# A rotary embedding on one core: three VectorE operations for five slabs, four stores as even and odd partitions, and a tile for each place of a slab

## The chip, the cores and the metric

The kernel runs on one core of a Trainium2 chip. The metric is the device time in microseconds (us) of one execution. Before the change it is 162.14 us, the median of three runs (162.01 to 162.23).

## The reference

`x` is float32 of 16 x 512 x 1024 (batch, sequence, dim): 33.5 MB to read, and as much to write. A row of 1024 is 16 heads of 64. In every head the first 32 numbers and the last 32 are turned against each other by tables that depend on the place in the sequence only:

```python
x = x.reshape(batch, seq, num_heads, head_dim)          # 16 x 512 x 16 x 64
x1, x2 = x[..., :half_dim], x[..., half_dim:]
cos = cos[None, :, None, :]                             # 512 x 32
sin = sin[None, :, None, :]
rotated = np.concatenate([x1 * cos - x2 * sin,
                          x1 * sin + x2 * cos], axis=-1)
```

## The kernel before

The work is cut into eight slabs of two batches, 4 MB each. A slab lies on 128 partitions with eight rows of 1024, so 32 KB of float32, on each. Slabs go in pairs: the two slabs of a pair take alternate runs of 32 KB in DRAM.

On chip, one tile `room` of 192 KB a partition holds six places ("slots") of one float32 slab each. `halves` is the same memory seen as bfloat16, so that a slot is also two halves (numbers 2i and 2i+1) which hold one bfloat16 slab each. Three tuples say where a slab lies: `land[s]` is the slot that its load fills, `home[s]` the half in which its bfloat16 form lies, `leave[s]` the slot from which it is stored as float32.

The steps of a slab:

- `load(s, r, n)` (L83) brings rows r to r+n of slab s into its slot, on SyncE's queue.
- `cast(s)` (L154) on ScalarE makes bfloat16 of it: `land` to `home`.
- `turn(s)` on VectorE does the arithmetic in bfloat16, for four of the eight rows at a time: a product of the swapped halves with the sine table into `turned_part`, a tile called `spare` in the profile (L168), a product with the cosine table in place (L168), and the sum in place (L171). That is six operations of 128 x 4096 for a slab.
- `spread(s)` (L158) on ScalarE makes float32 of it, `home` to `leave`, and then issues `store(s)` (L87), again on SyncE's queue. Slab 1 is spread and stored in two pieces of four rows.

The tables come in once: two loads of 64 KB, on ScalarE's queue, to 32 partitions four apart; GpSimd casts them, eight matmuls (L145) copy them to all partitions, and VectorE brings them from PSUM to bfloat16 (L150). They do not enter the loop again.

The order of the instructions on ScalarE, VectorE and SyncE is the order in the code (`tc.manual_schedule`). Loads 0 to 5 are issued at the start; load 6 goes to slot 2 after cast 2, load 7 (in pieces of six rows and two) to slot 3 after cast 3. Store 0 has a dependency of its own on load 7's first piece (`gate`), so that no store is under way before the loads are nearly through. All these transfers are on one queue, SyncE's.

Of the kernel before, what the change touches and what calls it, by code (L numbers as in the profile page):

```python
# [9 lines left out]
@with_exitstack  # L10
def kernel(
    ctx: ExitStack,
    tc: tile.TileContext,
    x: bass.AP,
    cos: bass.AP,
    sin: bass.AP,
    num_heads: int,
    out: bass.AP,
):
    nc = tc.nc  # L20
    P = nc.NUM_PARTITIONS

    batch, seq, dim = x.shape
    nh = num_heads
    hd = dim // nh
    half = hd // 2
    bf16 = mybir.dt.bfloat16
    f32 = mybir.dt.float32

    nb = 2  # L30
    slots = 6
    TAIL = 2
    nslabs = batch // nb
    G = 2
    rpp = nb * seq // P
    W = rpp * dim
    SP = seq // rpp
    TW = rpp * half

    out_flat = out.rearrange("b s h d -> b s (h d)")  # L40

    singles = ctx.enter_context(tc.tile_pool(name="singles", bufs=1))
    psum = ctx.enter_context(tc.tile_pool(
        name="psum", bufs=1, space=bass.MemoryType.PSUM))


    def dram(t, s, k):
        return bass.AP(tensor=t.tensor,
                       offset=t.offset + s // G * (G * nb * seq * dim) + s % G * W,
                       ap=[[G * W, P], [1, k * W]])  # L50


    def view(t, offset, *dims):
        return dataclasses.replace(t, offset=t.offset + offset,
                                   ap=[t.ap[0], *[list(d) for d in dims]])


    room = singles.tile([P, slots * W], f32, tag="room")
    halves = room.bitcast(bf16)


    land = (0, 1, 2, 3, 4, 5, 2, 3)
    home = (0, 1, 2, 3, 8, 9, 0, 1)
    leave = (5, 2, 5, 1, 2, 4, 5, 0)


    def rows(t, s, r, n):
        return bass.AP(
            tensor=t.tensor,
            offset=t.offset + s // G * (G * nb * seq * dim) + s % G * W + r * dim,  # L70
            ap=[[G * W, P], [1, n * dim]])


    def wide(slot, r, n):
        return view(room, slot * W + r * dim, (1, n * dim))


    def thin(s, r, n):
        return view(halves, home[s] * W + r * dim, (1, n * dim))


    def load(s, r, n):
        return nc.sync.dma_start(out=wide(land[s], r, n), in_=rows(x, s, r, n))  # L83


    def store(s, r, n):
        return nc.sync.dma_start(out=rows(out_flat, s, r, n), in_=wide(leave[s], r, n))  # L87

    TR = 32
    TQ = seq // TR // rpp
    TC = seq * half // TR
    spare = singles.tile([P, rpp // 2 * dim // 2], f32, tag="spare")
    turned_part = spare.bitcast(bf16)
    raw = view(spare, 0, (1, TC))
    nc.vector.memset(raw, 0.0)  # L97


    def load_tables(queue):  # L100
        for i, src in enumerate((cos, sin)):
            to = dataclasses.replace(
                raw, offset=raw.offset + i * raw.ap[0][0],
                ap=[[P // TR * raw.ap[0][0], TR], [1, TC]])
            queue.dma_start(out=to, in_=bass.AP(  # L105
                tensor=src.tensor, offset=src.offset, ap=[[TC, TR], [1, TC]]))


    load(0, 0, rpp)
    load_tables(nc.scalar)  # L110
    for s in range(1, slots):
        load(s, 0, rpp)

    GP = SP // G
    GT = G // TQ
    pick = singles.tile([P, 3 * GT * P], bf16, tag="pick")
    nc.gpsimd.memset(pick, 0.0)  # L119


    def selection(g, h):
        return pick[:, (g * GT + h // TQ) * P:(g * GT + h // TQ + 1) * P]


    for g in range(3):
        for h in range(0, G, TQ):
            part = view(selection(g, h), 0, (GP, P // GP), (1, GP))
            nc.gpsimd.affine_select(  # L129
                out=part, in_=part, compare_op=mybir.AluOpType.not_equal,  # L130
                fill=-1.0 if g == 2 else 1.0,
                base=-(1 if g else 0) - h // TQ * (P // TR),
                pattern=[[0, P // GP], [-(G // TQ) * (P // TR), GP]],
                channel_multiplier=1)

    raw_b = singles.tile([P, TC], bf16, tag="raw_b")
    nc.gpsimd.tensor_copy(out=raw_b, in_=raw)  # L137

    tab = {}


    def table(h):
        acc = psum.tile([P, 2 * rpp * hd], f32, tag=f"acc{h}")
        for g, at in ((0, 0), (0, half), (2, rpp * hd), (1, rpp * hd + half)):
            nc.tensor.matmul(  # L145
                view(acc, at, (hd, rpp), (1, half)), selection(g, h),
                view(raw_b, h % TQ * TW, (half, rpp), (1, half)),
                start=True, stop=True)
        tab[h] = singles.tile([P, 2 * rpp * hd], bf16, tag=f"tab{h}", name="tab")
        nc.vector.tensor_copy(out=tab[h], in_=acc)  # L150


    def cast(s, r=0, n=rpp):
        nc.scalar.copy(out=thin(s, r, n), in_=wide(land[s], r, n))  # L154


    def spread(s, r=0, n=rpp):
        nc.scalar.copy(out=wide(leave[s], r, n), in_=thin(s, r, n))  # L158
        return store(s, r, n)


    def turn(s):
        n = rpp // 2
        for r in (0, n):
            low = thin(s, r, n)
            flip = view(low, half, (hd, n * nh), (-half, 2), (1, half))
            for out_, in_, a in ((turned_part, flip, rpp * hd), (low, low, 0)):
                nc.vector.tensor_mul(  # L168
                    out=out_, in0=in_,
                    in1=view(tab[s % G], a + r * hd, (hd, n), (0, nh), (1, hd)))  # L170
            nc.vector.tensor_add(out=low, in0=low, in1=turned_part)  # L171


    with tc.manual_schedule(engines={
            mybir.EngineType.Activation, mybir.EngineType.DVE, mybir.EngineType.SP}):
        n = rpp // 2
        cast(0, 0, n)
        cast(0, n, n)
        for h in range(G):
            table(h)  # L180
        turn(0)
        cast(1)
        turn(1)
        cast(2)
        load(6, 0, rpp)
        turn(2)
        cast(3)
        gate = load(7, 0, rpp - TAIL)
        load(7, rpp - TAIL, TAIL)
        turn(3)  # L190
        cast(4)
        cast(5)
        first = spread(0)
        tc.add_manual_dep(
            first.ins, gate.ins.name,
            mybir.DependencyInfo(mybir.DependencyClass.Sync,
                                 mybir.DependencyReason.DATA),
            reason="behind the loads")
        turn(4)
        cast(6)  # L200
        spread(1, 0, n)
        spread(1, n, n)
        turn(5)
        spread(2)
        spread(3)
        spread(4)
        turn(6)
        cast(7)
        turn(7)
        spread(5)  # L210
        spread(6)
        spread(7)


# [33 lines left out]
```

## Time and profile before

| What | Before |
|---|---|
| Runs | 162.23, 162.01, 162.14 us; median 162.14 |
| The profiled execution | 162.36 us, with a span of 160.6 us: 1.8 us lie around the span |
| VectorE busy | 112.8 us (70%), 51 instructions |
| ScalarE busy | 113.5 us (71%), 19 instructions |
| TensorE, GpSimd busy | 1.9 us and 2.1 us |
| DMA | 67.25 MB, mean 419 GB/s over the span; SyncE's queue alone is 97.4% of what 16 DMA engines can be busy |
| Transfers on SyncE's queue | 9 for the loads, 9 for the stores |

The profile is of one execution. Its busy times are of instructions on the compute engines; transfers are counted apart, as packets on 16 DMA engines. The share of a transfer queue in the table is the time of its packets over 16 engines and the span, so that 100% means that every DMA engine had a packet at every moment. In a short window that share can come out over or under 1, since a packet counts in the window in which it starts.

### The profile page before, as it was taken

To read this page: it belongs to the slowest core of one execution; us is meant where nothing else is said; L and a number is where in the kernel's file an instruction comes from. 1 tells how busy PE (TensorE), PEld (TensorE's weight loads), DVE (VectorE), ACT (ScalarE), POOL (GpSimd) and SP (SyncE) were. 2 spreads that over 40 slices of the span, in tenths; PEclk is the share of its full clock that TensorE was granted. 3 is DMA by queue.
4 is the path that set the end of the run, shared out by engine and by line. 5 is a ranking of instruction groups with operands and counts; after the bars stand their busy time and mean duration, and the time that the engine had idled before them with its cause. 6 is when DMAs were issued, how large, how long until landed. Compare 5 with 4: busy or idle time off the path is not lost.

```text
span 160.6 us, 195 instructions
## 1 busy us (share of the span) xinstructions
PE 1.9 (1%) x8; PEld 1.1 (1%) x8; DVE 112.8 (70%) x51; ACT 113.5 (71%) x19; POOL 2.1 (1%) x9
## 2 busy tenths in 40 slices
PE   0004000000000000000000000000000000000000
PEld 0002000000000000000000000000000000000000
DVE  1002999999999999999999999999739990000000
ACT  3006949488493966999999799999999999800000
POOL 3001000000000000000000000000000000000000
DMA  7999999999999999999899999999999999999993
GB/s 261 408 408 408 506 392 392 498 416 392 490 424 392 473 441 392 457 392 465 375 506 416 392 441 473 392 433 482 392 433 475 392 416 498 392 392 514 400 392 139
DMA packets 2689, 67.25 MB, mean 419 GB/s; under 512 B 320, under 2 KB 320, under 8 KB 384
## 3 DMA queue, kind: packets, MB, share of 16 engines
q1 hardware_dynamic: 2592, 67.11, 97.4%
q10 hardware_dynamic: 96, 0.13, 0.2%
q14 instruction: 1, 0.01, 0.0%
HBM read 33.69 MB, written 33.55 MB: 419 GB/s over the span
## 4 chain that ended last, share of the span: by engine, by line
DVE 62%; ACT 13%; DMA 7%; issue 3%; PE 1%; POOLq 0%; ACTq 0%; DVEq 0%
DVE room L171 20%; DVE room L168 20%; DVE spare L168 20%; ACT room L158 9%; DMA spare<-in_sin_dram 7%; ACT room L154 4%; DVE tab L150 1%; PE acc L145 1%; POOLq L243 0%; ACTq L105 0%; DVE spare L97 0%; DVEq L168 0%; POOLq L137 0%; ACTq L158 0%
## 5 line engine op out<-in xcount | busy, mean ns | idle before, releaser
L154 ACT CAST room<-room 128x8192 bf16<-128x8192 f32 (+1 forms) x9 | 56.3, 6259 | 22.6 <-DMA room<-in_x_dram 22.5
L158 ACT CAST room<-room 128x8192 f32<-128x8192 bf16 (+1 forms) x9 | 56.0, 6258 | 1.3 <-DMA out_dram<-room 1.0
L168 DVE TENSOR_TENSOR spare<-room,tab 128x4096 bf16<-128x4096 bf16 x16 | 36.7, 2292 | 4.5 <-ACT room L154 3.6
L168 DVE TENSOR_TENSOR room<-room,tab 128x4096 bf16<-128x4096 bf16 x16 | 36.7, 2292 | 0.5
L171 DVE TENSOR_TENSOR room<-room,spare 128x4096 bf16<-128x4096 bf16 x16 | 36.7, 2292 | 0.5
L150 DVE CAST tab<-acc 128x1024 bf16<-128x1024 f32 x2 | 2.4, 1220 | 13.6 <-PE acc L145 13.6
L154 ACT ACT_TABLE_LOAD x1 | 1.3, 1283 | 2.6 <-issue 2.6
L145 PE MATMUL acc<-raw_b,pick 128*128 128x256 bf16 x8 | 1.9, 416 | 13.9 <-POOL raw_b L137 13.9
L145 PEld LDWEIGHTS <-pick 128*128 128x128 bf16 x8 | 1.1, 139 | 14.2 <-issue 12.2
L97 DVE MEMSET spare<- 128x512 f32 x1 | 0.5, 485 | 0.9 <-PEq L229 0.9
L129 POOL TENSOR_SCALAR_AFFINE_SELECT pick<-pick 128x128 bf16<-128x128 bf16 x3 | 0.8, 308 | 0.1
L137 POOL CAST raw_b<-spare 128x512 bf16<-128x512 f32 x1 | 0.6, 610 | 11.2 <-DMA spare<-in_sin_dram 11.2
L119 POOL MEMSET pick<- 128x384 bf16 x1 | 0.4, 417 | 0.3 <-POOLq L229 0.3
L229 POOL MEMSET const-bfloat16-1.0<- 128x1 bf16 x1 | 0.1, 101 | 0.0
L229 POOL MEMSET const-uint8-127<- 128x1 uint8 x1 | 0.1, 101 | 0.0
L229 POOL MEMSET const-float32-0.0<- 128x1 f32 x1 | 0.1, 98 | 0.2 <-issue 0.2
L229 POOL MEMSET const-float32-1.0<- 128x1 f32 x1 | 0.1, 98 | 0.0
## 6 DMA issues: line engine op xcount, KB each, us to landing
room<-in_x_dram SPq DMA_DIRECT2D x7, 4096.0 KB, 31.7
out_dram<-room SPq DMA_DIRECT2D x7, 4096.0 KB, 14.8
out_dram<-room SPq DMA_DIRECT2D x2, 2048.0 KB, 9.9
room<-in_x_dram SPq DMA_DIRECT2D x1, 3072.0 KB, 29.4
room<-in_x_dram SPq DMA_DIRECT2D x1, 1024.0 KB, 31.5
spare<-in_cos_dram ACTq DMA_DIRECT2D x1, 64.0 KB, 7.9
spare<-in_sin_dram ACTq DMA_DIRECT2D x1, 64.0 KB, 11.1
```

Source lines behind the costliest of these rows:

```text
L97: nc.vector.memset(raw, 0.0)
L119: nc.gpsimd.memset(pick, 0.0)
L129: nc.gpsimd.affine_select(out=part, in_=part, compare_op=mybir.AluOpType.not_equal, fill=-1.0 if g == 2 else 1.0, base=-(1 if g else 0) - ...
L137: nc.gpsimd.tensor_copy(out=raw_b, in_=raw)
L145: nc.tensor.matmul(view(acc, at, (hd, rpp), (1, half)), selection(g, h), view(raw_b, h % TQ * TW, (half, rpp), (1, half)), start=True, sto ...
L150: nc.vector.tensor_copy(out=tab[h], in_=acc)
L154: nc.scalar.copy(out=thin(s, r, n), in_=wide(land[s], r, n))
L158: nc.scalar.copy(out=wide(leave[s], r, n), in_=thin(s, r, n))
L168: nc.vector.tensor_mul(out=out_, in0=in_, in1=view(tab[s % G], a + r * hd, (hd, n), (0, nh), (1, hd)))
L171: nc.vector.tensor_add(out=low, in0=low, in1=turned_part)
L229: nc = _bacc.Bacc("TRN2", target_bir_lowering=False, num_devices=1)
```

## The change

- `room` becomes a list of six tiles, one a slot. `half_place(h, r, n)` gives rows of half h; the view of a slab in a slot or half is otherwise what it was.
- For slabs 0, 1, 2, 5 and 7 a free half, named in `aside`, takes the product of the swapped halves, and `turn` does all eight rows in three operations of 128 x 8192. Slabs 3, 4 and 6 keep `turned_part` and six operations.
- Since half 10, the first of slot 5, is slab 0's `aside`, load 5 is issued after `turn(0)`. Loads 6 and 7 change slots (3 and 2 for 2 and 3): load 6 stands behind cast 3, and load 7 behind `turn(2)`, which uses half 4 of slot 2. Cast 3 goes to half 3, which is slab 1's `aside`, so it stands behind `turn(1)`. `leave` changes for slabs 1 and 4, from slot 2 to slot 3.
- Cast 0 is one instruction of 128 x 8192 in place of two of 128 x 4096; in ScalarE's order, cast 3 now stands ahead of load 6, and casts 4 and 5 ahead of `turn(3)` in the code.
- `twice(s)` stores slabs 2, 3, 4 and 5 in two transfers each: partitions 0, 2, 4, ... and then 1, 3, 5, ... (64 each), with 32 KB for a partition as before. There are 13 transfers for the stores in place of 9.

```diff
-    room = singles.tile([P, slots * W], f32, tag="room")
-    halves = room.bitcast(bf16)
-    land = (0, 1, 2, 3, 4, 5, 2, 3)
+    room = [singles.tile([P, W], f32, tag=f"room{i}", name="room") for i in range(slots)]
+    halves = [t.bitcast(bf16) for t in room]
+    land = (0, 1, 2, 3, 4, 5, 3, 2)
     home = (0, 1, 2, 3, 8, 9, 0, 1)
-    leave = (5, 2, 5, 1, 2, 4, 5, 0)
+    aside = {0: 10, 1: 3, 2: 4, 5: 1, 7: 4}
+    leave = (5, 3, 5, 1, 3, 4, 5, 0)
...
+    def half_place(h, r, n):
+        return view(halves[h // 2], h % 2 * W + r * dim, (1, n * dim))
...
+    def every_other(t, i):
+        (step, count), rest = t.ap[0], t.ap[1:]
+        return dataclasses.replace(t, offset=t.offset + i * step,
+                                   ap=[[2 * step, count // 2], *rest])
+
+    def twice(s, r=0, n=rpp):
+        for i in (0, 1):
+            nc.sync.dma_start(out=every_other(rows(out_flat, s, r, n), i),
+                              in_=every_other(wide(leave[s], r, n), i))
...
-    for s in range(1, slots):
+    for s in range(1, slots - 1):
         load(s, 0, rpp)
...
     def spread(s, r=0, n=rpp):
         nc.scalar.copy(out=wide(leave[s], r, n), in_=thin(s, r, n))
-        return store(s, r, n)

     def turn(s):
-        n = rpp // 2
-        for r in (0, n):
+        n = rpp if s in aside else rpp // 2
+        for r in range(0, rpp, n):
             low = thin(s, r, n)
             flip = view(low, half, (hd, n * nh), (-half, 2), (1, half))
-            for out_, in_, a in ((turned_part, flip, rpp * hd), (low, low, 0)):
+            crossed = half_place(aside[s], 0, n) if s in aside else turned_part
+            for out_, in_, a in ((crossed, flip, rpp * hd), (low, low, 0)):
                 nc.vector.tensor_mul(
                     out=out_, in0=in_,
                     in1=view(tab[s % G], a + r * hd, (hd, n), (0, nh), (1, hd)))
-            nc.vector.tensor_add(out=low, in0=low, in1=turned_part)
+            nc.vector.tensor_add(out=low, in0=low, in1=crossed)
...
-        cast(0, 0, n)
-        cast(0, n, n)
         for h in range(G):
             table(h)
+        cast(0)
         turn(0)
+        load(5, 0, rpp)
         cast(1)
         turn(1)
         cast(2)
+        cast(3)
         load(6, 0, rpp)
         turn(2)
-        cast(3)
         gate = load(7, 0, rpp - TAIL)
         load(7, rpp - TAIL, TAIL)
-        turn(3)
         cast(4)
         cast(5)
-        first = spread(0)
+        turn(3)
+        spread(0)
+        first = store(0, 0, rpp)
...
         turn(4)
         cast(6)
-        spread(1, 0, n)
-        spread(1, n, n)
+        for r in (0, n):
+            spread(1, r, n)
+            store(1, r, n)
         turn(5)
-        spread(2)
-        spread(3)
-        spread(4)
+        for s in (2, 3, 4):
+            spread(s)
+            twice(s)
         turn(6)
         cast(7)
         turn(7)
-        spread(5)
-        spread(6)
-        spread(7)
+        for s in (5, 6, 7):
+            spread(s)
+            (twice if s == 5 else store)(s, 0, rpp)
```

4 lines of the change are left out of this document (2 added, 2 removed).

## The prediction, made before the changed kernel ran

> **What bounds the kernel now.** I read the page first: the two rows of engines, the slices, the DMA queues.
>
> ```profile
> DVE  1002999999999999999999999999739990000000
> ACT  3006949488493966999999799999999999800000
> ...
> DMA  7999999999999999999899999999999999999993
> ...
> q1 hardware_dynamic: 2592, 67.11, 97.4%
> q10 hardware_dynamic: 96, 0.13, 0.2%
> q14 instruction: 1, 0.01, 0.0%
> ```
>
> VectorE (DVE) and ScalarE (ACT) stop five to seven slices of 4 us before the end; the DMA engines are full from the second slice to the last but one. SyncE's queue q1 fills 97.4% of the span. q14 is a packet of none of the kernel's transfers, an instruction fetch, and will matter. The page's chain of work that ended last reads "DVE 62%", which misleads: its last piece is ScalarE's cast at 132.92, 7.02 us long. It follows instructions and ends 20 us early. What ends last is a transfer, as SyncE's own waits say:
>
> ```profile
> SPq L87 <- ACT room L158: 58.1, 8, 13.5
> ...
> SPq L87 <- DMA room<-in_x_dram: 28.6, 1, 28.6
> SPq L243 <- DMA out_dram<-room: 19.2, 1, 19.2
> ```
>
> The last line is the end of the program (L243), which waits 19.2 us for the last store. The stores' waits for ScalarE (58.1 us) cost nothing while the queue still has packets. Whether it always has is seen by stage, with windows cut where loads end (81.2) and store 3 lands (119.9); the last two numbers are the DMA share and GB/s.
>
> ```profile
> 0.50:81.20 80.70, 1.87 (x8) 1.11 (x8) 65.48 (x31) 55.97 (x10) 1.86 (x5) 1.00 0.99 424
> 81.20:119.90 38.70, 0.00 (x0) 0.00 (x0) 34.52 (x16) 37.67 (x8) 0.00 (x0) 1.00 1.01 434
> 119.90:159.50 39.60, 0.00 (x0) 0.00 (x0) 12.76 (x6) 19.84 (x3) 0.00 (x0) 1.00 0.95 411
> ```
>
> Two equal amounts of work: stores 0 to 3 in 38.7 us, stores 4 to 7 in 39.6. The lost 0.9 us has an owner. Each DMA engine takes a row of 32 KB in 1213 ns, one after the other, so that a 4 MB slab is eight rows deep, 9.7 us. At 120.92 one engine also takes the fetch, an 8192 byte packet of 309 ns, and its rows on both sides take 1516 and 1571 ns. It stays behind: of store 4's 16 completion counts, 15 are in at 129.55, the last at 130.53; of the last store's, 158.66 and 159.49. So 15 engines idle for the final 0.83 us. The rest is 1.74 us until the first packet, and 1.1 us from the last count to the end of the span. Nothing else is left to gain.
>
> **The change, part by part.** The profiled execution took 162.36 us, 0.22 over the median.
>
> *VectorE's three operations.* The rows by shape:
>
> ```profile
> L154 ACT CAST room<-room 128x8192 bf16<-128x8192 f32 x7 | 49.1, 7018 | 13.2 <-DMA room<-in_x_dram 13.1
> ...
> L171 DVE TENSOR_TENSOR room<-room,spare 128x4096 bf16<-128x4096 bf16 x16 | 36.7, 2292 | 0.5
> ...
> L154 ACT CAST room<-room 128x4096 bf16<-128x4096 f32 x2 | 7.2, 3605 | 9.4 <-DMA room<-in_x_dram 9.4
> ```
>
> No 8192 operation of VectorE is shown. Above, it is two of 2292 ns, 4.58 us; below, ScalarE's ratio for the same two sizes (7018/3605 = 1.95) gives 4.46. I take 4.46, as the double size is what both share. A slab is then 3 x (4.46 + 0.03 between) = 13.5 us for 6 x 2.325 = 13.95: 0.45 us on each of five slabs, 2.3 us in all, and none of it on the path, since the queue sets the end. So the times by which transfers can be issued must be walked through for loss. Cast 0 whole: 13.29 + 7.02 = 20.3 (turn 0 began at 17.23). Turns 0, 1, 2 end at 33.9, 47.4, 60.9. Load 5 now waits for turn 0, with load 6 and all else queued behind it on SyncE: issued at 33.9, and the queue has load 4 until 51.95. Cast 3 waits for turn 1 (its half): 47.4 to 54.5; load 6 follows at 54.5, the queue lasts to 61.66. Loads 7 wait for turn 2: 60.9 against 71.4. Casts 4 (to 61.5) and 5 (data at 61.66) are then where they were, and with them ScalarE's whole later order; store 0 still goes out at 78.7 at its gate. Turn 5 must wait for the half that spread 1 frees at 90.0 (VectorE is there at 88.9), ends at 103.5, turn 6 at 117.5; turn 7 begins when cast 7 ends, 118.9, and ends at 132.4, before ScalarE is free for spread 7 at 132.8. Stores 2 to 7 go out as now at 98.0, 105.1, 112.0, 125.8, 132.8 and 140.0, against queue ends of 100.6, 110.2, 119.9, 129.2, 138.8 and 148.5. From issue to first packet took 1.01 us at the start (0.73 to 1.74). The thinnest cover is store 2's: 2.5 less 1.0, so 1.5 us. The sum for all this is 0; if a step is later than its cover, what goes beyond it is added to the end.
>
> *Fewer instructions.* VectorE issues 15 fewer. Who asked for the fetch at 120.92? SyncE had issued nothing since 112.4. ScalarE's cast at 118.78 is the 33rd of its 40 records in the trace, VectorE's product at 118.91 the 59th of 68. I take VectorE: if the engines' programs are cut alike, only it comes as far as 59. Its 68 become about 53 and it never gets there, unless six or more new waits are recorded as instructions of their own (now it has about a dozen). Saved: the final lag, 0.83 us; 0 if it was ScalarE's, which keeps 39. [...]
>
> *Stores 2 to 5 in two transfers.* Four more issues on SyncE, 0.33 us each, behind a wait for ScalarE and 2.5 us or more ahead of need: 0. One more completion packet of 9 ns per engine for each, 0.04 us. Semaphores recur after eight transfers, so later ones wait for earlier ones to have landed: the tightest is store 5's, which need store 1 (100.6) at 125.8. The speed of 64 partitions two apart is the open cost. Nearest rows: store 1 in two pieces, 4.83 us each, so a split alone is free; and the table loads, 32 partitions four apart on all 16 engines: every 2 KB packet 84 ns, and the 32 KB rows around them still 1213. I take 1213 ns, because those packets show spaced partitions with no delay, to them or to their neighbours; the other end (two engines at one group of partitions, half speed) is +38.6, below. A gain below 1213 is excluded: that is the time of a row in loads and stores, split or whole, alike.
>
> *The tail.* After the last count SyncE goes through five waits on pairs of semaphores, 0.065 us apart, and the last store's stands first. With 13 stores it falls on the eighth semaphore, whose pair stands last: 0 to 0.26 us saved; I take the middle, 0.13. Six tiles for one move no byte: 0, unless a wait comes with it that the covers above don't hold.
>
> Sum: 162.36 - 0.83 - 0.13 + 0.04 = 161.44 for a profiled execution, less 0.22 for the median: **161.2 us** (alone, 160.9 to 161.6).
>
> **The rivals.** (a) *Even and odd partitions share readers; slower.* If the 64 rows are dealt to the engines four in order, an engine reads partitions 8j, 8j+2, 8j+4, 8j+6 in place of eight of its own. Should partitions be served in groups, neighbours meet at one group in step, and each row takes up to 2 x 1213 ns. Four stores then last 19.3 us each: 161.2 + 4 x 9.66 = 199.8; meeting half of the time, 180.5. It decides early: 2.4% more per row (1242 ns) eats the whole gain. For it: no transfer of half the partitions is in the trace, and nothing waits behind these stores that could hide it. Against it: the 84 ns packets, though they are short. [...]
>
> (b) *The fetch stays* (ScalarE asked, or VectorE's waits refill the count): 162.14 - 0.13 + 0.04 = 162.05, no change. For it: ScalarE's cast began within 0.13 us of VectorE's product.
>
> (c) *A small loss*: a wait that the tiles bring, or SyncE's longer program fetching too. One more fetch beside a kept one: 162.1 + 0.8 = 162.9; a store late by 2 us beyond its cover, 164.
>
> **How the numbers follow.** Forecast 0.52; (b) 0.12; (c) 0.10; (a) 0.26, of which 0.08 up to half of the meeting and 0.18 beyond. About 0.2% (0.32 us) is what a measurement of this kernel can tell from no change, so faster 0.52, same 0.12, slower 0.36. The range goes from the forecast's low end less the rounding, 160.8, through (b), (c) and the milder part of (a), to 181: 0.82. What is left out is full sharing.
>
> **What would show it.** q14 gone from the page; the last stage (stores 4 to 7) at 38.7 us and 434 GB/s; all 16 counts of the last store within 0.5 us, near 158.7; VectorE at 36 busy instructions, 8192 ones near 4.46 us; rows of stores 2 to 5 still 1213 ns. I am wrong if these rows are longer, if the fetch is there, or if a slice before the end shows the DMA engines idle.

## The result, and the profile after

The changed kernel takes 161.38 us, the median of six runs (161.22 to 161.88), against 162.15 (162.01 to 162.23). The ratio is 0.9957, with a 95% interval of 0.9942 to 0.9971: 0.43% faster. The forecast was 161.2. The profiled execution took 161.30 us with a span of 159.5; before it was 162.36 and 160.6. Ratios leave disturbed runs out, which matters for one experiment below only: with partitions 0 to 63 and 64 to 127 the ratio is that of the two runs at 197.2 us, and the other four, the profiled one among them, took 200.3 to 201.5.

The page after, with the DMA row and the queues:

```profile
DMA  7999999999999999999999999999999999999995
...
q1 hardware_dynamic: 2656, 67.11, 98.1%
q10 hardware_dynamic: 96, 0.13, 0.2%
HBM read 33.69 MB, written 33.55 MB: 422 GB/s over the span
```

The line of q14 is not there: no instruction fetch falls into the span. Queue q1 has 64 packets more (2656 for 2592), the completion packets of four more transfers on 16 engines, and fills 98.1% of a shorter span. The windows, cut at the same three places (loads done, store 3 landed, last store landed; columns as before, DMA share and GB/s last):

```profile
0.50:81.30 80.80, 1.86 (x8) 1.09 (x8) 63.16 (x22) 55.67 (x9) 1.86 (x5) 1.00 0.99 423
81.30:120.00 38.70, 0.00 (x0) 0.00 (x0) 34.67 (x13) 37.68 (x8) 0.00 (x0) 1.00 1.01 434
120.00:158.70 38.70, 0.00 (x0) 0.00 (x0) 12.28 (x3) 19.83 (x3) 0.00 (x0) 1.00 0.97 420
```

Stores 4 to 7 now take 38.7 us, as stores 0 to 3 do, where before they took 39.6. The loads take what they took (80.8 us for 80.7). The span is shorter by 1.06 us, and two numbers make that up: the last completion count comes at 158.69 instead of 159.49 (0.80), and the end of the span follows it by 0.83 us instead of 1.08 (0.25). SyncE's own waits show the second part:

```profile
SPq L88 <- DVE room L188: 36.2, 2, 30.4
SPq L103 <- ACT room L175: 30.2, 4, 11.8
SPq L92 <- ACT room L175: 22.1, 4, 7.4
SPq L262 <- DMA out_dram<-room: 18.2, 2, 9.6
```

The closing wait (L262, L243 before) was one wait of 19.2 us. Now it is two that sum to 18.2: the earlier closing waits are through while the last stores are still under way, and only the wait on the last store's own pair of semaphores, which stands last, is left at the end. In the trace the five closing waits of the kernel before run one behind the other from 159.51 to 159.79 us, all after the last count; in the changed kernel three stand at 140.3 to 140.4, the fourth ends when store 6 lands (149.0), and only the fifth comes after the last count, at 158.71. The first line is new and harmless: loads 5 and 7 wait for VectorE's sum (L188), 30.4 us for load 5, and no slice above shows the DMA engines idle for it. VectorE's rows by shape:

```profile
L185 DVE TENSOR_TENSOR room<-room,tab 128x8192 bf16<-128x8192 bf16 x10 | 44.2, 4424 | 6.9 <-ACT room L171 4.7 <-ACT room L175 2.0
L188 DVE TENSOR_TENSOR room<-room 128x8192 bf16<-128x8192 bf16 x5 | 22.1, 4425 | 0.2
```

An operation of 128 x 8192 takes 4424 ns, under twice 2292.

### The profile page after: what moved, and what is told of

The parts are those of the page before. It is cut to its first block, busy times and chain, and to the rows that moved or that the text cites. A ratio compares the mean times of both kernels' runs of the same rounds, so it can differ in the third digit from the quotient of the medians.

```text
span 159.5 us, 178 instructions
## 1 busy us (share of the span) xinstructions
PE 1.9 (1%) x8; PEld 1.1 (1%) x8; DVE 110.1 (69%) x36; ACT 113.2 (71%) x18; POOL 2.1 (1%) x9
## 3 DMA queue, kind: packets, MB, share of 16 engines
q1 hardware_dynamic: 2656, 67.11, 98.1%
## 4 chain that ended last, share of the span: by engine, by line
ACT 28%; DMA 27%; DVE 20%; issue 13%; ACTq 0%; SPq 0%
ACT room L175 24%; DMA room<-in_x_dram 19%; DVE room L185 17%; DMA out_dram<-room 8%; ACT room L171 4%; DVE room L188 3%; ACTq L171 0%; SPq L92 0%; ACTq L175 0%
## 5 line engine op out<-in xcount | busy, mean ns | idle before, releaser
L171 ACT CAST room<-room 128x8192 bf16<-128x8192 f32 x8 | 56.0, 7017 | 22.9 <-DMA room<-in_x_dram 15.6
L185 DVE TENSOR_TENSOR room<-room,tab 128x8192 bf16<-128x8192 bf16 (+1 forms) x16 | 58.0, 3624 | 7.1 <-ACT room L171 4.7
L188 DVE TENSOR_TENSOR room<-room 128x8192 bf16<-128x8192 bf16 x5 | 22.1, 4425 | 0.2
L188 DVE TENSOR_TENSOR room<-room,spare 128x4096 bf16<-128x4096 bf16 x6 | 13.8, 2293 | 0.2
L185 DVE TENSOR_TENSOR spare<-room,tab 128x4096 bf16<-128x4096 bf16 x6 | 13.7, 2289 | 0.2
```

Source lines behind the costliest of these rows:

```text
L185: nc.vector.tensor_mul(out=out_, in0=in_, in1=view(tab[s % G], a + r * hd, (hd, n), (0, nh), (1, hd)))
L188: nc.vector.tensor_add(out=low, in0=low, in1=crossed)
```

## The experiments

Two theories had to be told apart. Mine: the gain is the fetch that no longer happens (VectorE's shorter program) and the shorter closing waits (the number of stores); even and odd partitions cost nothing and bring nothing else. The rivals: the split itself helps the DMA engines; or ScalarE's program, also three records shorter, removed the fetch. (A record is an entry that the trace has for an engine; its waits on semaphores count as records too.)

**The three operations without the split.** The changed kernel with

```diff
-            twice(s)
+            store(s, 0, rpp)
...
-            (twice if s == 5 else store)(s, 0, rpp)
+            store(s, 0, rpp)
```

> The changed kernel with stores 2 to 5 whole again (9 transfers for the stores). Theory (fetch and tail apart): no packet on q14 within the span, so the last store's 16 counts within 0.5 us near 158.7, but the last store's semaphore stands first among the five closing waits again, which gives back 0.25 us: a span near 159.75 and a median near 161.6. Rival (the split itself brings the gain, by the DMA engines): the last count back at 159.5 and 162.1. Rival (the three operations alone bring all): 161.4.

Measured: 161.57 us, ratio 0.9973 (0.9963 to 0.9983), no packet on q14. In its trace the last count comes at 158.75 and the end of the span 1.08 us later: the fetch's part stays, the tail's part goes back. So the split is not what removes the late engine, and the three operations do not bring all. The second point rests on the trace: by the medians alone the interval overlaps that of the changed kernel (0.9942 to 0.9971).

**The split without the three operations.** The kernel before with six tiles, `twice` for stores 2 to 5, and six operations of 128 x 4096 for every slab.

> The kernel before with six tiles and with stores 2 to 5 as even and odd partitions; VectorE keeps six operations for each slab. Theory: the fetch stays, near 120.9, one DMA engine ends 0.8 us behind the others, but the closing waits take 0.25 us less: a median near 161.9, 0.15% under before. Rival (the split brings the gain): 161.4 with no late engine.

Measured: 161.82 us, ratio 0.9988 (0.9976 to 1.0000). Its page has the fetch, and its closing wait the new form:

```profile
q14 instruction: 1, 0.01, 0.0%
```

```profile
SPq L256 <- DMA out_dram<-room: 18.4, 2, 9.6
```

The end of the span follows the last count by 0.82 us, so the tail is shortened by the number of stores alone. (By the medians the 0.18 us is at the edge of what can be told: the interval ends at 1.0000.) The late engine is late by only 0.22 us here (158.99 against 158.77 for the fifteenth count), which was not expected and is taken up below. By medians, the two halves of the change bring 0.43 and 0.18 us against runs of the kernel before on the same chip; the whole brought 0.77 and, when run again, 0.76.

**Rows instead of partitions.** The changed kernel with stores 2 to 5 split into two pieces of four rows on all partitions:

```diff
-        for i in (0, 1):
-            nc.sync.dma_start(out=every_other(rows(out_flat, s, r, n), i),
-                              in_=every_other(wide(leave[s], r, n), i))
+        for q in (0, rpp // 2):
+            store(s, q, rpp // 2)
```

> The changed kernel, but stores 2 to 5 split into rows 0 to 3 and rows 4 to 7 of all 128 partitions instead of even and odd partitions; 13 transfers for the stores as there. Theory (what the split brings is only the place of the last store's semaphore): as the changed kernel, 161.4, with no fetch and with the last count near 158.7. Rival (even and odd partitions matter by themselves): 161.7 or more.

Measured: 161.67 us, ratio 0.9977 (0.9966 to 0.9988). It is not the expected tie by medians, although the interval touches that of the changed kernel; it lies near the rival's 161.7. The closing is the short one (0.83 us after the last count); what is later is the last count, 159.07 for 158.69. Packets are 16 KB here, 611 ns each by the median, so 1222 for 32 KB where a whole row takes 1213. With eight rows deep and four stores that is 4 x 8 x 9 ns = 0.29 us, an estimate that covers most of the 0.38 us by which the last count is later. So, by that estimate, even and odd partitions are the cheaper way to have two transfers, because their packets stay whole; the medians alone do not part the two.

**Low and high partitions.** The changed kernel with partitions 0 to 63 and 64 to 127 for even and odd:

```diff
-        return dataclasses.replace(t, offset=t.offset + i * step,
-                                   ap=[[2 * step, count // 2], *rest])
+        return dataclasses.replace(t, offset=t.offset + i * (count // 2) * step,
+                                   ap=[[step, count // 2], *rest])
```

> The changed kernel, but the two transfers of stores 2 to 5 are partitions 0 to 63 and 64 to 127. Theory (groups of partitions have one reader's worth of speed, and 64 neighbours reach half of the groups): rows of these four stores at up to 2 x 1213 ns, each store up to 19.3 us, 161.4 + 38.6 = 200.0. Rival (a row is limited by its DMA engine alone): 1213 ns and 161.4, as for even and odd partitions.

Measured: 197.2 us, ratio 1.2173 (1.2145 to 1.2201); the profiled execution took 200.32 us. Windows from it for the stage before stores 2 to 5, and for these four stores:

```profile
81.20:100.60 19.40, 0.00 (x0) 0.00 (x0) 17.27 (x6) 18.37 (x5) 0.00 (x0) 1.00 1.04 432
100.60:178.40 77.80, 0.00 (x0) 0.00 (x0) 29.76 (x10) 39.17 (x6) 0.00 (x0) 1.00 0.99 248
```

The DMA engines are as busy as ever (0.99) and move a little over half as much: the four stores take 77.8 us for 38.6. Rows that took 1213 ns take 2547 by the median of the window from 100.6 to 130 us; they differ widely (1213 to 5256 ns), and later in the stage more of them take 1213 again. The price that rival (a) of the prediction gave, +38.6 us, is near what was paid: 39.0 us more than the changed kernel in the profiled executions, 35.8 by the medians. So which half of the partitions a transfer takes decides whether it is paid (161.38 us with every other one, 197.2 with neighbours). Nothing in the busy share tells of it; the GB/s (248 for 435) and the packet's time do. The theory's groups of partitions, each with one reader's speed, are a supposition: 2547 ns here and 1213 in the changed kernel fit it, but no row shows such a group, nor where the rows meet. A different half of the partitions is also a different set of DRAM addresses written at the same time, and no run changes one without the other.

**More instructions on VectorE.** The changed kernel with n one-column memsets on VectorE near the start, where it waits for the tables: 8 and 20 (in a tile of 32 columns), then 40.

```diff
     load_tables(nc.scalar)
+    idle = singles.tile([P, 64], f32, tag="idle")
+    for i in range(n):
+        nc.vector.memset(idle[:, i:i + 1], 0.0)
```

> The changed kernel with 8 more instructions on VectorE, one-column memsets of a tile of their own near the start, where VectorE waits for the tables anyway. Its recorded instructions become 57, of which 54 come before the end. Theory (VectorE's program crosses a block at its 59th or 60th record): no fetch, as the changed kernel, 161.4. Rival (the threshold lies lower): the fetch is back and costs 0.8 us.

> The changed kernel with 20 such memsets: 69 recorded instructions, one more than the kernel before. Theory: an 8192 byte packet on q14 is back within the span, when VectorE comes to its 59th record (near 95 us); one DMA engine ends about 0.8 us behind the others: 162.2. Rival (ScalarE asked for the fetch before, and what removed it was ScalarE's shorter program): no fetch, 161.4.

> The changed kernel with 40 one-column memsets more on VectorE near the start, 89 recorded instructions. With 20 more the fetch came at 119.58, beside VectorE's 63rd record at 118.97, and not near 95 us. Theory (the place in VectorE's program decides): with 20 more in front the same place is reached 20 records earlier, near 60 to 65 us, and the packet is there; 161.4 to 162.2. Rival (the fetch is tied to VectorE's wait at 115 to 119 us or to that time): again near 119 to 121 us.

Measured: with 8 more, 161.59 us and no fetch (0.9972, 0.9960 to 0.9983). With 20 more, 161.83 (162.2 was expected) with the fetch at 119.58 (0.9984, 0.9973 to 0.9994). With 40 more, 162.03 with the fetch at 60.01, half the kernel earlier (0.9999, 0.9986 to 1.0011). From a window of 59.9 to 60.4 us of the last one, the queues; and from its timeline, the product that VectorE had next:

```profile
q14 instruction: 1, 0.01, 4.0%
```

```profile
60.15 2.28 DVE L188 TENSOR_TENSOR spare<-room,tab 128x4096 bf16<-128x4096 bf16 x1
```

That product is VectorE's 60th record. In the kernel before, the fetch came at 120.92 beside records 59 and 60; with 20 memsets, beside the 63rd. So the place in VectorE's program decides, not the time, and the forecast of 95 us for 20 more (59th record) was off by four records; why the count differs by that much, and whether a block of the program ends there, as the expectation for 8 memsets had it, the traces do not show. With 8 more, 57 records in all, the place isn't reached. ScalarE has 37 records in all three runs, so its shorter program is not what removed the fetch.

Two things were not expected. With 8 more the time is 0.25 us over the changed kernel's 161.34 on the same chip, with no fetch to explain it, and in its profiled execution one count comes 0.41 us behind the fifteenth all the same. Why stays open. And with 40 more nearly the whole gain is gone, though the closing waits are still short (0.83 us). There the fetch falls among the loads, and the trace shows what it holds up: one engine's share of load 5 lands at 62.65, where the others are done by 61.70; the first piece of load 7 lands at 79.70 for 78.78; and store 0, whose gate is that piece, is issued at 79.75 for 78.83. The other engines run dry for a moment: none begins a row of store 0 before 80.60, where in the changed kernel they begin one by one from 80.29. In the profiled execution the fifteenth count of the last store then comes at 159.11 for 158.63. How much of that 0.48 us is the gate's is not shown: the changed kernel, run again, had it at 159.08 in its profiled execution, with no fetch.

**More instructions on ScalarE.** The changed kernel with 34 one-column copies on ScalarE, while it waits for the first load.

```diff
     load_tables(nc.scalar)
+    idle = singles.tile([P, 64], f32, tag="idle")
+    nc.gpsimd.memset(idle, 0.0)
+    for i in range(34):
+        nc.scalar.copy(out=idle[:, i + 1:i + 2], in_=idle[:, 0:1])
```

> The changed kernel with 34 one-column copies more on ScalarE while it waits for the first load, 71 recorded instructions there and 49 on VectorE. Theory (each engine has such a place of its own at about the same count): a packet on q14 is back, near ScalarE's 60th to 64th record, about 119 us; up to 0.8 us slower than the changed kernel, 161.4 to 162.2. Rival (only VectorE's program is long enough ahead of the records): no packet, 161.4.

Measured: 161.57 us, ratio 0.9968 (0.9955 to 0.9980), and a fetch at 105.94, beside ScalarE's 61st record at 105.19. From a window of 105.5 to 106.5 us:

```profile
q14 instruction: 1, 0.01, 1.9%
```

So each of the two engines has such a place, at about the same count, and ScalarE's 40 records before the change could not have reached its own. That settles whose fetch it was. The forecast had the record right, and its time (about 119 us) wrong. The twelve profiled executions agree: those with 68 or more records on VectorE, or 71 on ScalarE, have a fetch within the span, and those with 57 or fewer on VectorE and 37 on ScalarE have none. Here the last count (158.83) comes level with the fifteenth (158.80), and little was lost. By my estimate the struck DMA engine was ahead of the others; the trace does not name it.

**Six tiles alone**, and **the changed kernel again**, on the chip of the runs with 8 and 20 memsets:

> The kernel before with the six places of a slab as tiles of their own and nothing else. Theory: not a byte and not a wait changes on the path: 162.15, with the fetch. Rival (tiles change waits): a time off by more than 0.3 us.

> The changed kernel itself, on the chip of these runs, for comparison: 161.4, no fetch. Every theory expects the same.

Measured: 162.10 us, ratio 1.0001 (0.9992 to 1.0010), with the fetch at 120.74; and 161.34, ratio 0.9951 (0.9935 to 0.9968), with none. The tiles are worth nothing by themselves. None of the variants beat the changed kernel.

## Why the prediction was right

- *VectorE's time is not on the path.* An 8192 operation was put at 4.46 us and took 4.42. VectorE's 2.6 us of work less (112.76 to 110.12) shows nowhere in the time.
- *The walk through the covers.* Turns 0, 1 and 2 were to end at 33.9, 47.4, 60.9 and ended at 33.8, 47.0, 60.3. Loads 5, 6 and 7 were put at 33.9, 54.5, 60.9 and were issued at 33.8, 54.1, 60.3. Stores 2 to 7 were put at 98.0, 105.1, 112.0, 125.8, 132.8 and 140.0; they went out at 98.1, 105.2, 112.1, 125.9, 132.8 and 139.9. Turn 7 ended at 132.3 (132.4). Every cover held, so the sum for all this was 0, as said. But they were thinner than the walk had them. It reckoned them up to the last engine's count, and the first engine comes free about 1 us earlier: in the changed kernel store 0's first row begins at 80.29, and the last count of the loads is in at 81.26. Less the 0.85 us from issue to first row that the run with 40 memsets shows (79.75 to 80.60), an estimated 0.6 us was left to store 0 (issued at 78.83), which the walk did not name, and about as much to store 2, where it said 1.5.
- *The fetch*: said -0.83 in a profiled execution, measured -0.80. VectorE's records went from 68 to 49 (said 53). But for the median this term was too large. The run without the split, which has this part alone, is 0.43 us under the kernel before. By my estimate the price of a fetch depends on how far ahead the DMA engine is that carries it; the trace does not name that engine, so this is not shown. The struck engine loses 0.5 to 1.0 us at once (the fetch and what the rows beside it take over 1213 ns), but the 16 engines end 0.3 to 0.8 us apart anyway (the executions without a fetch, partitions 0 to 63 left out), and one that was ahead would lose less. Behind the fifteenth count, the last was late by 0.83 us before, and by 0.22, 0.61, 0.76, 0.43 and 0.03 in the five profiled executions of experiments that have the fetch; without one it was 0.04 to 0.41 (again without partitions 0 to 63). The 0.83 came from one execution, and is the largest of the six.
- *The tail*: 0 to 0.26 was given, 0.13 taken; it was 0.25, the upper end. The reason held: the closing waits go by pairs, and the last store's pair moved from the first place (159.51) to the last (158.71).
- *The split*: rows 1213 ns, as taken; the completion packets 9 ns each. The issues were mis-sized: 0.33 us was said for each, and they took 0.47 to 1.39, which the cover hid. The tightest recurrence of a semaphore was misread: store 4's second half, issued at 112.6, needs store 0 (91.0), 21.6 us to spare, less than store 5's 25; neither is near the path.
- *The sum*: 161.44 for a profiled execution, measured 161.30; 161.2 for the median, measured 161.38. That the median comes so close is in part luck. The fetch's term is too large by some 0.4 for the median and the tail's too small by 0.12, so the two partly cancel; and the 0.22 us taken off supposed that a profiled execution lies over the median, where the changed kernel's lies 0.08 under it. What is left is within the 0.66 us by which the six runs differ.
- *The rivals*: (a) has about the right price, but for other partitions than these; its mechanism, partitions served in groups, fits the 2547 ns and is not shown. The 84 ns packets of the table loads were the right row to go by. (b) fell with the fetch. Of (c) nothing was seen: SyncE's 43 records for 38 brought no fetch, and no cover gave out.

The fetch shows as no stall on the engine that asks: in the kernel before, VectorE's product that begins at 118.91 ends at 121.20, and the next begins at 121.24. It has a price all the same, as the end of this kernel is set by the slowest of 16 full DMA engines (there the last count comes at 159.49, the fifteenth at 158.66): on one chip the medians are 161.83 with a fetch (20 memsets) against 161.59 (8 memsets) and 161.34 (none) without one, so the price is 0.2 to 0.5 us, by which of the two it is reckoned from.

## What to carry to other kernels

When the DMA engines are full from end to end, as here, compute is not worth shortening for its time (2.6 us less on VectorE showed nowhere), but its instructions may be worth removing, for some tenths of a microsecond (0.2 to 0.5 here): look for a queue of instruction fetches within the span. One completion count behind the rest is a hint, not a proof; with 8 memsets it was there without a fetch (0.41 us). Then read the end of the program like any other chain: which wait comes last, and what is left in line behind it. If a transfer has to be cut in two, keep the packets whole and take every other partition, not the lower and upper half (161.38 us against 197.2 here).

## What was not expected of the hardware

- Partitions 0 to 63 as one transfer: a 32 KB row takes 2547 ns by the median of the window from 100.6 to 130 us, about twice 1213, with the DMA share unchanged (0.99).
- Issuing a transfer of every other partition took SyncE 0.47 to 1.39 us, against 0.33 for one of all 128 that stands alone:

```profile
L92 SPq DMA_DIRECT2D out_dram<-room x5: 332/338/347, 78.8 to 139.9; - x5
```

```profile
L103 SPq DMA_DIRECT2D out_dram<-room x8: 471/560/1386, 98.1 to 126.4; - x8
```

  These are the minimum, median and maximum in ns, from the changed kernel's answers for the two lines that issue stores (L92 whole, L103 by halves). The first half of each pair took 0.47 to 0.54, the second 0.58 to 1.39. With half of low or high partitions it was up to 2.65. The long ones are not a matter of every other partition: in the run by rows, with all 128, the second of each pair took 0.83 to 1.24.

```profile
L92 SPq DMA_DIRECT2D out_dram<-room x13: 332/332/1244, 78.7 to 139.8; - x13
```

  They go with standing right behind another issue. Why that takes longer stays open.
- A fetch of 8192 bytes costs its DMA engine one and a half to three times its own 309 ns, since rows beside it also take longer: 1516 and 1571 ns in the kernel before, one of 1582 to 1589 in three of the experiments, one of 1373 with the copies on ScalarE, one of 1875 with 40 memsets.
